# Token-layout projections of 512 columns and score products of 128 rows in a two-block attention network

## The chip, the cores and the metric

The kernel runs on one core of a Trainium2 chip. Its time is the device time of one execution in microseconds (us). The engines are TensorE (PE, matmuls; PEld its weight loads), VectorE (DVE), ScalarE (ACT), GpSimd (POOL) and SyncE (SP, which issues nearly all DMAs). All run side by side, each in its own order, and wait for one another by semaphores.

## The reference

The input is one sequence of 512 tokens with 1024 channels. Two different blocks of two layers each follow one another. Cut to what matters here:

```python
# first block, per layer
h = x @ w_in[i]                       # q, k, v of three attentions, and three gates
o_fox = fox_attention(fq, fk, fv, log_f)       # 6 heads of 64, a cumulated forget gate in the logits
o_sb  = stick_breaking_attention(sq, sk, sv)   # 5 heads of 64
o_dsa = dsa_attention(dq, dk, dv, iq, ik, iw)  # 5 heads of 64, on the 256 best keys
merged = gates0 * (o_fox @ w_up_fox[i]) + gates1 * (o_sb @ w_up_sb[i]) + gates2 * (o_dsa @ w_up_dsa[i])
x = layer_norm(ALPHA * x + merged @ w_out[i])
ffn = square(relu(x @ w_ff_in[i])) @ w_ff_out[i]               # 4096 hidden channels
ple = sigmoid(x @ w_ple_gate[i]) * (p[i] @ w_ple[i])
x = layer_norm(ALPHA * x + ffn + ple)
# second block, per layer
mixed = concatenate([y_nsa * silu(z_nsa), y_lru * silu(z_lru), y_conv * silu(z_conv)])   # 3 x 512 channels
x = x + mixed @ w_out_2[l]                                     # then an RMS norm
```

In the forget-gate attention the logits of query q and key k are `q.k / 8 + c[q] - c[k]`, where c is the running sum of the log gates.

## The kernel before, in words

Every operand of a large matmul is held as two tiles, a rounded high part and the low remainder. `mm3` (L209) multiplies high by high, high by low and low by high into one PSUM bank, so each k-tile of 128 channels takes three passes (L212 to L214).

Two layouts are in use. In the channel layout (`w_tiles`, L239) 128 columns of the weight stand in the array and all 512 tokens move, so each pass has 512 columns. In the token layout (`t_groups`, L262) 128 tokens of the activation stand in the array and the weight's columns move. A group of columns is loaded as slabs of four k-tiles by 256 columns (`slab`, L216), split by ScalarE and VectorE or GpSimd (`wsplit`, L235), and then each block of 128 tokens goes through all k-tiles before the next block starts.

The token layout serves five places: the attention output (`out1`, L822), the side gate and its partner `w_ple` (L876 to L891), the four chunks of the feed-forward output (L924), and the second block's output (`out2`, L1510). In all of them 1024 output columns are taken in four quarters of 256. `out_groups` (L858) takes the first two quarters one by one and the last two together, so that the last two share one walk over the token blocks and the norm of block b can start when block b is done. The residual tile of a quarter comes from `quarter` (L855). VectorE adds each quarter from PSUM, takes its statistics (`bn_stats`), and behind the last quarter `norm_out` (L795) norms the block and transposes it for the next stage.

The score products are in `scores` (L312): `q` and `k` are lists of operands that are multiplied pairwise. `head_pairs` (L534) makes them for the forget-gate and stick-breaking heads. A query tile holds the high part in 64 rows and the low part in the other 64 (`query_stack`, L417), a key tile the high part twice (`key_stack`, L434), and the key's low part is a separate half tile of 64 rows, two heads to a tile (`low`). So one pass has 128 rows and a second one has 64. The forget gate adds a third product between them, of 38 rows (L731). Where an attention has five heads, the up-projection of `branch` (L669) has a last k-tile of 64 channels: it takes one pass of 128 rows (L693, the weight's high part above its low part) and one of 64 rows (L694).

The program is written in order of dependence; the framework orders each engine's instructions itself, by a simulated time line, and mixes stages where data and buffers allow. The numbers of buffers are fixed in `BUFS` (L89) and `PBUFS` (L107): 13 `qk` tiles in the first block, four `wh` and four `wl` slabs, four `raw` slabs, and PSUM banks under the names `mm` (3), `ss` (2), `tr` (2), `av` and `acc` (1 each). `ORDER` (L103) gives the stages of a first-block layer: index, selection, forget-gate project, sparse project, forget-gate attend, best keys, sparse attend, branch of the forget gate (x), stick-breaking project and attend, and the branches of sparse (z) and stick-breaking (y).

Of the kernel before, what the change touches and what calls it, by code (L numbers as in the profile page):

```python
# [11 lines left out]
F32 = mybir.dt.float32  # L12
# [18 lines left out]
def _shape_constants():  # L31
# [14 lines left out]
    for h in range(6):  # L46
        sel[h::32, h] = 1.0
    cast = [mask(i[None, :] <= i[:, None]), mask(i[None, :] // 64 <= i[:, None] // 64),
# [21 lines left out]
class Net:  # L70
# [26 lines left out]
    COMMON = ["wh", "wl"]  # L97
    WORDS = dict(s=512, rs=512, tmp=256, raw=1024, wh=1024, wl=1024)
    SIDE = 9
# [162 lines left out]
    def t_groups(self, w, groups, x, emit, K=KD, ks=4, first=None, then=None):  # L262
# [6 lines left out]
        for b in range(NT):  # L269
            tok = slice(b * P, (b + 1) * P)  # L270
            for g, cols in enumerate(groups):
# [9 lines left out]
                emit(b, g, ps[:, :n])  # L281


    def transpose_block(self, src, b, xh, xl, kd=KD):
# [149 lines left out]
    def key_stack(self, ps, z, lo, r):  # L434

        nc = self.nc
        hi = z[r:r + 64]
        nc.scalar.activation(hi, ps[r:r + 64], AF.Copy)
        self.lo_engine().tensor_sub(lo, ps[r:r + 64], hi.bitcast(F32))
        nc.scalar.activation(z[64 - r:128 - r], ps[r:r + 64], AF.Copy)  # L440

    def index_project(self, w, x, then):
# [91 lines left out]
    def head_pairs(self, w, tiles, x):  # L534


        q, k, lows = {}, {}, []

        def low(j):
            if j % 2 == 0:  # L540
                lows.append(self.t("qk", [P, 2, T], F32R))
            return lows[-1][:, j % 2]

        def emit(i, ps):
            j = i // 2
            ps = self.staged(ps)
            t = self.t("qk", [P, 2, T], F32R)
            if i % 2 == 0 and i == len(tiles) - 1:
                z, l = t[:, 0], low(j)[:64]
                self.query_stack(ps, z, 0, 0)  # L550
                self.key_stack(ps, t[:, 1], l, 64)
                q[2 * j], k[2 * j] = (z, z[:64]), (t[:, 1], l)
                return
            l = low(j) if i % 2 else None
            for r in range(2):
                rows, h = slice(64 * r, 64 * r + 64), 2 * j + r
                z = t[:, r]
                if i % 2:
                    self.key_stack(ps, z, l[rows], 64 * r)
                    k[h] = z, l[rows]  # L560
                else:
                    self.query_stack(ps, z, 64 * r, 64 * r)
                    q[h] = z, z[rows]

        self.w_tiles(w, tiles, x, emit)
        return q, k
# [66 lines left out]
    def attend(self, n_heads, v, probs):  # L633


        pairs = []
        for j in range((n_heads + 1) // 2):
            o = self.t("os", [P, T])
            nr = min(2, n_heads - 2 * j)
            for r in range(nr):  # L640
                h = 2 * j + r
                for half in range(2):
                    av = self.ps("av")[:, :256]
                    self.unit(half, lambda b, s, p: probs(h, b, s, p), v(h), av)
# [24 lines left out]
    def branch(self, w, g0, wup, pairs, rows, x, emit):  # L669
# [6 lines left out]
        def gate(f, ps):  # L676
# [25 lines left out]
    def mix1(self, i, x, then=None):  # L702
# [88 lines left out]
    def stats(self):  # L791

        return [self.small([P, 4, 6]) for _ in range(NT)]

# [27 lines left out]
    def out1(self, i, merged, xd):  # L822
# [10 lines left out]
        def add(j):  # L833
            def emit(b, k, ps):
                v = self.quarter(y, b, j + k)
                nc.vector.scalar_tensor_tensor(v, v, ALPHA, ps, op0=OP.mult, op1=OP.add)
                nc.vector.bn_stats(st[b][:, j + k], v)
                if j + k == 3:
                    self.norm_out(y[b], b, st[b], g, bb, 1e-5, x)
            return emit  # L840

        self.out_groups(a["w_out"][i], m, add)
        return x, y
# [9 lines left out]

    @staticmethod
    def quarter(y, b, j):  # L855
        return y[b][j // 2][:, j % 2 * 256:j % 2 * 256 + 256]

    def out_groups(self, w, x, add, K=KD):  # L858
# [14 lines left out]
    def ffn(self, i, x, y, pt, post=None):  # L873
        nc = self.nc
        a = self.a
        for j in range(4):  # L876
            cols = [(j * 256, 256)]
            wh, wl = self.wpair(self.slab(a["w_ple"][i], cols, 0, 2))

            def emit(b, ps):  # L880
                s = self.t("tmp", [P, 256])
                nc.scalar.activation(s, ps, AF.Tanh, scale=0.5)
                u = self.ps("mm")[:, :256]
# [4 lines left out]
                v = self.quarter(y, b, j)  # L888
                nc.vector.scalar_tensor_tensor(v, v, ALPHA, s, op0=OP.mult, op1=OP.add)

            self.t_group(a["w_ple_gate"][i], cols, x, emit)  # L891
        xo = self.xpair()
        xn = self.dram([T, D])
        nch = 4
        for ch in range(nch):
# [18 lines left out]
            def add(j):  # L914
                def emit(b, k, ps):
                    v = self.quarter(y, b, j + k)
                    nc.vector.tensor_add(v, v, ps)
                    if last:
                        nc.vector.bn_stats(st[b][:, j + k], v)
                    if last and j + k == 3:  # L920
# [589 lines left out]
    def out2(self, l, mixed, xd):  # L1510
# [10 lines left out]
        def add(j):  # L1521
            def emit(b, k, ps):
                v = self.quarter(y, b, j + k)
                nc.vector.tensor_add(v, v, ps)
                nc.vector.bn_stats(st[b][:, j + k], v)
                if j + k == 3:
                    rows = slice(b * P, (b + 1) * P)
# [10 lines left out]
        self.lo_on_pool = False  # L1538
        for j in range(4):
            self.t_groups(a["w_out"][l], [[(j * 256, 256)]], m, add(j), K=12)  # L1540
        return h, xn
# [77 lines left out]
```

## Time and profile before

| what | value |
|---|---|
| median of 3 runs | 2654.8 us (2652.48 to 2656.91) |
| profiled execution, its own time | 2650.83 us |
| its span, first to last instruction | 2649.0 us |
| mean granted TensorE clock in the span | 0.98 of 2.4 GHz |
| busy: PE, DVE, ACT, POOL | 97%, 62%, 45%, 29% |
| PE instructions | 15636 |
| DMA, mean | 89 GB/s |

All times below are from the one profiled execution, counted from its first instruction. A row of the time line gives the start in us, the duration in us, engine, line, operation, tiles (`out<-in`), the form (rows*columns of the array, then the moving operand) and how many instructions of the kind follow one another. Matmuls are pipelined and their ends are modelled: the price of one is read from the starts, not from the durations. A stretch of the view by windows gives the busy time of each engine, its instructions in brackets, the granted clock of TensorE (1.00 is 2.4 GHz, 0.50 is 1.2 GHz), the share of the DMA engines and GB/s.

### The profile page before, as it was taken

To read this page: it belongs to the slowest core of one execution; us is meant where nothing else is said; L and a number is where in the kernel's file an instruction comes from. 1 tells how busy PE (TensorE), PEld (TensorE's weight loads), DVE (VectorE), ACT (ScalarE), POOL (GpSimd) and SP (SyncE) were. 2 spreads that over 40 slices of the span, in tenths; PEclk is the share of its full clock that TensorE was granted. 3 is DMA by queue.
4 is the path that set the end of the run, shared out by engine and by line. 5 is a ranking of instruction groups with operands and counts; after the bars stand their busy time and mean duration, and the time that the engine had idled before them with its cause. 6 is when DMAs were issued, how large, how long until landed. Compare 5 with 4: busy or idle time off the path is not lost.

```text
span 2649.0 us, 40689 instructions
## 1 busy us (share of the span) xinstructions
PE 2577.2 (97%) x15636; PEld 2272.5 (86%) x15636; DVE 1651.1 (62%) x3306; ACT 1179.9 (45%) x2229; POOL 765.5 (29%) x853
## 2 busy tenths in 40 slices
PE   8999999999999999999999999998999989999988
PEld 8878878989988987787799889988987679988678
DVE  4975665643344669657565443346699765699764
ACT  5655543232233255555323332233675742566750
POOL 6621352000000264205100000004596322587330
PEclk9989999999999998999999999999999999999999
DMA  5202225232233332122432323133512034522140
GB/s 168 74 15 75 78 68 172 84 110 90 80 104 96 103 82 66 45 81 63 135 120 85 112 93 114 58 109 105 136 45 70 27 101 125 143 68 68 34 141 33
DMA packets 256642, 236.84 MB, mean 89 GB/s; under 512 B 23168, under 2 KB 245696, under 8 KB 256448
## 3 DMA queue, kind: packets, MB, share of 16 engines
q1 hardware_dynamic: 256448, 234.25, 29.5%
q8 instruction: 123, 2.02, 0.3%
q14 instruction: 71, 0.58, 0.1%
HBM read 224.51 MB, written 9.70 MB: 88 GB/s over the span
## 4 chain that ended last, share of the span: by engine, by line
PE 85%; DVE 10%; ACT 3%; issue 1%; POOL 1%; DMA 0%; DVEq 0%; POOLq 0%; SPq 0%; ACTq 0%
PE mm L212 24%; PE mm L213 24%; PE mm L214 24%; PE ss L317 3%; PE av L367 3%; PE tr L352 2%; DVE acc L1350 1%; DVE s L324 1%; PE tr L360 1%; DVE sc L492 1%; PE ss L731 1%; PE tr L413 1%; DVE m L491 1%; PE av L1178 1%; PE mm L694 1%
## 5 line engine op out<-in xcount | busy, mean ns | idle before, releaser
L236 ACT ACTIVATE wh<-raw 128x1024 fp32r<-128x1024 f32 (+3 forms) x418 | 414.2, 995 | 553.7 <-PE mm L214 372.7
L212 PE MATMUL mm<-xt,wh 128*128 128x512 f32 x1456 | 576.6, 396 | 7.2 <-ACT sig L1394 4.9
L213 PE MATMUL mm<-xt,wh 128*128 128x512 f32 x1456 | 576.6, 396 | 0.0
L214 PE MATMUL mm<-xt,wl 128*128 128x512 f32 x1456 | 573.1, 394 | 0.0
L237 DVE TENSOR_TENSOR wl<-raw,wh 128x1024 fp32r<-128x1024 f32 (+3 forms) x312 | 374.5, 1202 | 208.8 <-ACT wh L236 203.9
L213 PE MATMUL mm<-wl,qk 128*128 128x256 f32 x1728 | 485.7, 283 | 0.0
L214 PE MATMUL mm<-wh,qk 128*128 128x256 f32 x1728 | 485.2, 283 | 0.0
L212 PE MATMUL mm<-wh,qk 128*128 128x256 f32 x1728 | 485.0, 284 | 0.0
L213 PEld LDWEIGHTS mm<-wl,qk 128*128 128x128 f32 x1728 | 330.3, 192 | 0.5
L212 PEld LDWEIGHTS mm<-xt,wh 128*128 128x128 f32 x1456 | 276.0, 190 | 63.7 <-ACT sig L1394 5.4
L214 PEld LDWEIGHTS mm<-wh,qk 128*128 128x128 f32 x1728 | 330.5, 192 | 0.0
L212 PEld LDWEIGHTS mm<-wh,qk 128*128 128x128 f32 x1728 | 329.6, 192 | 0.5
L214 PEld LDWEIGHTS mm<-xt,wl 128*128 128x128 f32 x1456 | 275.6, 189 | 56.4 <-issue 1.6
L213 PEld LDWEIGHTS mm<-xt,wh 128*128 128x128 f32 x1456 | 276.1, 190 | 55.4 <-issue 1.8
L299 POOL TENSOR_SCALAR tiny<-tiny 128x1 f32<-128x1 f32 x24 | 13.3, 554 | 1002.0 <-DVE tiny L801 982.5
L237 POOL TENSOR_TENSOR wl<-raw,wh 128x1024 fp32r<-128x1024 f32 (+7 forms) x106 | 233.0, 2205 | 159.1 <-ACT wh L236 157.0
L212 PE MATMUL mm<-wh,xt 128*128 128x256 f32 (+5 forms) x880 | 263.0, 304 | 6.5 <-ACT wh L236 6.4
L214 PE MATMUL mm<-wh,xt 128*128 128x256 f32 (+6 forms) x880 | 264.4, 302 | 3.8 <-DVE xt L205 3.8
L213 PE MATMUL mm<-wl,xt 128*128 128x256 f32 (+6 forms) x880 | 265.5, 304 | 1.8 <-DVE wl L237 1.2
L212 PEld LDWEIGHTS mm<-wh,xt 128*128 128x128 f32 x880 | 169.6, 195 | 9.0 <-ACT wh L236 6.4
L214 PEld LDWEIGHTS mm<-wh,xt 128*128 128x128 f32 x880 | 170.5, 194 | 5.6 <-DVE xt L205 4.4
L213 PEld LDWEIGHTS mm<-wl,xt 128*128 128x128 f32 x880 | 170.8, 194 | 4.5 <-DVE wl L237 1.7
(321 smaller groups left out, 4181.5 us busy)
## 6 DMA issues: line engine op xcount, KB each, us to landing
raw<-in_w_in SPq DMA_DIRECT2D x84, 512.0 KB, 3.8
raw<-in_w_ff_in SPq DMA_DIRECT2D x64, 512.0 KB, 4.9
raw<-in_w_ff_out SPq DMA_DIRECT2D x64, 512.0 KB, 3.5
raw<-in_w_in SPq DMA_DIRECT2D x104, 256.0 KB, 3.3
raw<-in_w_out SPq DMA_DIRECT2D x40, 512.0 KB, 3.9
raw<-in_w_ple_gate SPq DMA_DIRECT2D x16, 512.0 KB, 4.1
raw<-in_cmp_w SPq DMA_DIRECT2D x16, 512.0 KB, 5.0
spill<-ac SPq DMA_DIRECT2D x24, 256.0 KB, 2.1
```

The source lines that it names most:

```text
L212: mm(out, A[0], B[0], start=start, stop=False)
L213: mm(out, A[0], B[1], start=False, stop=False)
L214: mm(out, A[1], B[0], start=False, stop=stop)
L236: self.nc.scalar.activation(hi, raw, AF.Copy)
L237: (self.nc.gpsimd if self.lo_on_pool else self.nc.vector).tensor_sub(lo, raw, hi.bitcast(F32))
L317: self.nc.tensor.matmul(s, u[:, tok], v[:, :n], start=i == 0, stop=i == len(k) - 1)
L324: nc.vector.tensor_tensor_reduce(p, s, bias, -0.125, 3e38, OP.add, OP.min, m)
L352: nc.tensor.transpose(tr[:, kb * P:(kb + 1) * P], p[:, kb * P:(kb + 1) * P], self.ident)
L360: nc.tensor.transpose(tr[:, i * P:(i + 1) * P], src, self.ident)
L367: nc.tensor.matmul(av[:, 256 - m.shape[-1]:], v[:, kb], m, start=start and kb + i == 0, stop=stop and kb == n - 1 and i == 1)
L413: nc.tensor.transpose(tr[:, i * P:(i + 1) * P], z[:, i].rearrange("p a d -> p (a d)"), self.identr)
L491: nc.vector.max(m8, sc)
```

## The change

The token layout gets a new walk, `wide`. It takes 512 columns at a time, slabs of two k-tiles by 512 columns, and one PSUM bank for each of the four token blocks (the banks named in `WIDE`). The first k-pairs are walked with the pair outside and the four blocks inside; the last `stay` pairs are held together and walked block by block, and each block is emitted when it is done. `out_halves` replaces `out_groups`: the first half of the columns with one pair held, the second with four. For eight k-tiles four pairs are all, so the second half is walked block by block in the `mm` banks. The side gate and `w_ple` take two halves as well. The adds and statistics on VectorE take 512 columns at once, the tile of the side gate comes from `sig` instead of `tmp`, and `quarter` is gone.

The second operand of the scores is made 128 rows high: `key_stack` copies the low part of the key into the other 64 rows too, and the second product takes the whole query tile. Each head now has a key tile of its own beside the query tile that two heads share. The forget-gate product takes all 128 rows, with a selector that has ones at two rows only. The last k-tile of an up-projection with five heads takes 128 rows in both passes; its `pairs` tile gets high and low parts copied into the lower half. The words of a `ph` tile go from 384 to 512.

```diff
     sel = np.zeros((P, 6))
     for h in range(6):
-        sel[h::32, h] = 1.0
+        sel[[h, 32 + h], h] = 1.0
...
-    WORDS = dict(s=512, rs=512, tmp=256, raw=1024, wh=1024, wl=1024)
+    WORDS = dict(ph=512, s=512, rs=512, tmp=256, raw=1024, wh=1024, wl=1024)
...
+    WIDE = ("av", "ss", "ss", "tr")
+
+    def wide(self, w, c0, x, emit, K=KD, stay=4):
+        pairs = list(range(0, K, 2))
+        first, last = pairs[:-stay], pairs[-stay:]
+        cols = [(c0, T)]
+        banks = [self.ps(t) for t in self.WIDE] if first else None
+
+        def add(ps, b, k0, slab):
+            tok = slice(b * P, (b + 1) * P)
+            h, l = slab
+            for k in (k0, k0 + 1):
+                self.mm3(ps, (x[0][:, k, tok], x[1][:, k, tok]), (h[:, k - k0], l[:, k - k0]), k == 0, k == K - 1)
+
+        for k0 in first:
+            slab = self.wpair(self.slab(w, cols, k0, 2))
+            for b in range(NT):
+                add(banks[b], b, k0, slab)
+        slabs = [self.wpair(self.slab(w, cols, k0, 2)) for k0 in last]
+        for b in range(NT):
+            ps = banks[b] if first else self.ps("mm")
+            for k0, slab in zip(last, slabs):
+                add(ps, b, k0, slab)
+            emit(b, ps)
...
         nc.scalar.activation(hi, ps[r:r + 64], AF.Copy)
-        self.lo_engine().tensor_sub(lo, ps[r:r + 64], hi.bitcast(F32))
+        self.lo_engine().tensor_sub(lo[r:r + 64], ps[r:r + 64], hi.bitcast(F32))
         nc.scalar.activation(z[64 - r:128 - r], ps[r:r + 64], AF.Copy)
+        nc.scalar.activation(lo[64 - r:128 - r], lo[r:r + 64].bitcast(F32), AF.Copy)
...
+        def pair():
+            t = self.t("qk", [P, 2, T], F32R)
+            return t[:, 0], t[:, 1]
 
         def emit(i, ps):
             j = i // 2
             ps = self.staged(ps)
...
+            if i % 2:
+                for r in range(2):
+                    k[2 * j + r] = pair()
+                    self.key_stack(ps, *k[2 * j + r], 64 * r)
                 return
...
+            z = pair()
+            last = i == len(tiles) - 1
+            for r in range(1 if last else 2):
+                self.query_stack(ps, z[r], 64 * r, 64 * r)
+                q[2 * j + r] = z[r], z[r]
+            if last:
+                k[2 * j] = pair()
+                self.key_stack(ps, *k[2 * j], 64)
...
             if nr == 1:
-                self.nc.scalar.activation(t[64:, 0], t[:64, 0].bitcast(F32), AF.Copy)
+                self.nc.scalar.activation(t[64:], t[:64].bitcast(F32), AF.Copy)
...
-                nc.tensor.matmul(u, h[:64, full, c], pairs[full][:64, 1], start=False, stop=False)
+                nc.tensor.matmul(u, h[:, full, c], pairs[full][:, 1], start=False, stop=False)
...
-                    r = slice(64 * (h % 2), 64 * (h % 2) + 38)
-                    nc.tensor.matmul(s, self.sel[r, h:h + 1].to_broadcast([38, P]), c[r, :n],
+                    nc.tensor.matmul(s, self.sel[:, h:h + 1].to_broadcast([P, P]), c[:, :n],
                                      start=False, stop=False)
...
-        cols = [[(j * 256, 256)] for j in range(4)]
-        for j in range(2):
-            self.t_groups(w, [cols[j]], x, add(j), K)
-        self.t_groups(w, cols[2:], x, add(2), K)
+    def out_halves(self, w, x, add, K=KD):
+
+        self.wide(w, 0, x, add(0), K, stay=1)
+        self.wide(w, T, x, add(1), K)
...
-            self.t_group(a["w_ple_gate"][i], cols, x, emit)
+            self.wide(a["w_ple_gate"][i], j * T, x, emit, stay=1)
...
-            self.out_groups(a["w_ff_out"][i][ch * D:(ch + 1) * D], m, add)
+            self.out_halves(a["w_ff_out"][i][ch * D:(ch + 1) * D], m, add)
...
-        for j in range(4):
-            self.t_groups(a["w_out"][l], [[(j * 256, 256)]], m, add(j), K=12)
+        self.out_halves(a["w_out"][l], m, add, K=12)
```

## Rows read from the trace of the kernel before

**Rows 1.** The page, busy time by engine and the chain that ended last.

```profile
PE 2577.2 (97%) x15636; PEld 2272.5 (86%) x15636; DVE 1651.1 (62%) x3306; ACT 1179.9 (45%) x2229; POOL 765.5 (29%) x853
...
PE 85%; DVE 10%; ACT 3%; issue 1%; POOL 1%; DMA 0%; DVEq 0%; POOLq 0%; SPq 0%; ACTq 0%
```

**Rows 2.** Busy time by stretch: engines, granted clock, DMA share, GB/s.

```profile
440.00:900.00 460.00, 460.00 (x3153) 429.86 (x3152) 218.59 (x327) 133.92 (x173) 9.23 (x12) 1.00 0.31 96
100.00:130.00 30.00, 30.00 (x157) 25.51 (x155) 28.83 (x77) 15.80 (x41) 17.03 (x24) 1.00 0.30 84
131.00:159.00 28.00, 27.57 (x89) 20.72 (x90) 23.18 (x71) 11.97 (x34) 5.68 (x11) 0.51 0.00 1
159.00:190.00 31.00, 30.69 (x160) 23.21 (x160) 18.92 (x58) 17.33 (x44) 6.03 (x12) 1.00 0.10 30
285.00:360.00 75.00, 75.00 (x368) 58.20 (x367) 56.41 (x91) 41.25 (x93) 41.71 (x63) 1.00 0.20 56
```

**Rows 3.** PE by line and form: count, busy us, mean ns, idle before.

```profile
L212 PE MATMUL mm<-xt,wh 128*128 128x512 f32 x1456 | 576.6, 396 | 7.2 <-ACT sig L1394 4.9 <-DVE sig L1314 1.8 <-DVE cg L1385 0.6
...
L213 PE MATMUL mm<-wl,qk 128*128 128x256 f32 x1728 | 485.7, 283 | 0.0
...
L694 PE MATMUL mm<-qk,wh 64*128 64x512 f32 x32 | 15.9, 497 | 0.0
...
L317 PE MATMUL ss<-qk,qk 64*128 64x512 f32 x22 | 10.6, 481 | 0.0
```

**Rows 4.** PE in order of time, from the up-projections into the attention output.

```profile
439.95 0.39 PE L212 MATMUL mm<-qk,wh 128*128 128x512 f32 x1
...
440.63 0.28 PE L212 MATMUL mm<-wh,qk 128*128 128x256 f32 x1
...
445.90 0.28 PE L214 MATMUL mm<-wh,qk 128*128 128x256 f32 x1
```

**Rows 5.** PE in order of time, an up-projection and a stick-breaking score pair.

```profile
299.55 0.39 PE L693 MATMUL mm<-qk,wh 128*128 128x512 f32 x1
299.87 0.50 PE L694 MATMUL mm<-qk,wh 64*128 64x512 f32 x1
300.29 0.92 PE L317 MATMUL ss<-qk,qk 128*128 128x512 f32 x2
301.15 0.50 PE L212 MATMUL mm<-qk,wh 128*128 128x512 f32 x1
301.48 0.39 PE L213 MATMUL mm<-qk,wh 128*128 128x512 f32 x1
```

**Rows 6.** PE in order of time, token layout with 448 columns.

```profile
96.71 0.36 PE L212 MATMUL mm<-wh,xt 128*128 128x448 f32 x1
...
98.94 0.37 PE L214 MATMUL mm<-wh,xt 128*128 128x448 f32 x1
```

**Rows 7.** PE in order of time, forget-gate scores; L731, L317 and L212 lie between.

```profile
176.11 0.40 PE L317 MATMUL ss<-qk,qk 128*128 128x512 f32 x1
...
177.43 0.39 PE L213 MATMUL mm<-qk,wh 128*128 128x512 f32 x1
```

**Rows 8.** PE in order of time, sparse scores, two products of 128 rows.

```profile
196.68 0.62 PE L317 MATMUL ss<-q,q 128*128 128x512 f32 x2
197.14 0.27 PE L360 MATMUL tr<-kept,s 128*128 128x128 f32 x1
```

**Rows 9.** ACT and POOL by line and form, key copies of the forget-gate heads.

```profile
L440 ACT ACTIVATE qk<-s 64x512 fp32r<-64x512 f32 x12 | 7.6, 630 | 0.3
...
L439 POOL TENSOR_TENSOR qk<-s,qk 64x512 fp32r<-64x512 f32 x12 | 15.5, 1291 | 1.2 <-ACT qk L438 0.8
```

**Rows 10.** DVE in order of time, the last add of the kernel.

```profile
2641.74 0.42 DVE L1524 TENSOR_TENSOR ac<-ac,mm 128x256 f32<-128x256 f32 x1 [0.52 <-PE mm L214]
```

**Rows 11.** The page, weight splits: mean ns, idle before and its releaser.

```profile
L236 ACT ACTIVATE wh<-raw 128x1024 fp32r<-128x1024 f32 (+3 forms) x418 | 414.2, 995 | 553.7 <-PE mm L214 372.7
...
L237 DVE TENSOR_TENSOR wl<-raw,wh 128x1024 fp32r<-128x1024 f32 (+3 forms) x312 | 374.5, 1202 | 208.8 <-ACT wh L236 203.9
```

More of the change, by code (lines that the diff above doesn't have):

```diff
@@ L534, in head_pairs @@
     def head_pairs(self, w, tiles, x):
[L537 to L542, printed above, removed]
+        q, k = {}, {}
+        def pair():
+            t = self.t("qk", [P, 2, T], F32R)
+            return t[:, 0], t[:, 1]
         def emit(i, ps):
@@ L546, in emit @@
             ps = self.staged(ps)
[L547 to L552, printed above, removed]
-                return
[L554 to L563, printed above, removed]
+            if i % 2:
+                for r in range(2):
+                    k[2 * j + r] = pair()
+                    self.key_stack(ps, *k[2 * j + r], 64 * r)
+                return
+            z = pair()
[6 more added lines that the diff above has]
+                self.key_stack(ps, *k[2 * j], 64)
         self.w_tiles(w, tiles, x, emit)
@@ L791, in stats @@
     def stats(self):
-        return [self.small([P, 4, 6]) for _ in range(NT)]
+        return [self.small([P, 2, 6]) for _ in range(NT)]
     def norm_out(self, y, b, stats, g, bb, eps, x, xd=None, post=None):
@@ L833, in add, with emit @@
         def add(j):
-            def emit(b, k, ps):
-                v = self.quarter(y, b, j + k)
+            def emit(b, ps):
+                v = y[b][j]
                 nc.vector.scalar_tensor_tensor(v, v, ALPHA, ps, op0=OP.mult, op1=OP.add)
-                nc.vector.bn_stats(st[b][:, j + k], v)
-                if j + k == 3:
+                nc.vector.bn_stats(st[b][:, j], v)
+                if j == 1:
                     self.norm_out(y[b], b, st[b], g, bb, 1e-5, x)
             return emit
-        self.out_groups(a["w_out"][i], m, add)
+        self.out_halves(a["w_out"][i], m, add)
         return x, y
@@ L852, in residual @@
         return y
[L854 to L858, printed above, removed]
-        cols = [[(j * 256, 256)] for j in range(4)]
-        for j in range(2):
-            self.t_groups(w, [cols[j]], x, add(j), K)
-        self.t_groups(w, cols[2:], x, add(2), K)
+    def out_halves(self, w, x, add, K=KD):
+        self.wide(w, 0, x, add(0), K, stay=1)
+        self.wide(w, T, x, add(1), K)
     def ple_input(self, i):
@@ L875, in ffn @@
         a = self.a
-        for j in range(4):
-            cols = [(j * 256, 256)]
-            wh, wl = self.wpair(self.slab(a["w_ple"][i], cols, 0, 2))
+        ple = {}
+        for j in range(2):
             def emit(b, ps):
-                s = self.t("tmp", [P, 256])
+                if b == 0:
+                    ple[j] = self.wpair(self.slab(a["w_ple"][i], [(j * T, T)], 0, 2))
+                wh, wl = ple[j]
+                s = self.t("sig", [P, T])
                 nc.scalar.activation(s, ps, AF.Tanh, scale=0.5)
-                u = self.ps("mm")[:, :256]
+                u = self.ps("mm")
                 tok = slice(b * P, (b + 1) * P)
@@ L887, in emit @@
                 nc.vector.scalar_tensor_tensor(s, s, 1.0, u, op0=OP.add, op1=OP.mult)
-                v = self.quarter(y, b, j)
+                v = y[b][j]
                 nc.vector.scalar_tensor_tensor(v, v, ALPHA, s, op0=OP.mult, op1=OP.add)
-            self.t_group(a["w_ple_gate"][i], cols, x, emit)
+            self.wide(a["w_ple_gate"][i], j * T, x, emit, stay=1)
         xo = self.xpair()
@@ L914, in add, with emit @@
             def add(j):
-                def emit(b, k, ps):
-                    v = self.quarter(y, b, j + k)
+                def emit(b, ps):
+                    v = y[b][j]
                     nc.vector.tensor_add(v, v, ps)
                     if last:
-                        nc.vector.bn_stats(st[b][:, j + k], v)
-                    if last and j + k == 3:
+                        nc.vector.bn_stats(st[b][:, j], v)
+                    if last and j == 1:
                         self.norm_out(y[b], b, st[b], g, bb, 1e-5, xo, xn, post)
                 return emit
-            self.out_groups(a["w_ff_out"][i][ch * D:(ch + 1) * D], m, add)
+            self.out_halves(a["w_ff_out"][i][ch * D:(ch + 1) * D], m, add)
         return xo, xn
@@ L1521, in add, with emit @@
         def add(j):
-            def emit(b, k, ps):
-                v = self.quarter(y, b, j + k)
+            def emit(b, ps):
+                v = y[b][j]
                 nc.vector.tensor_add(v, v, ps)
-                nc.vector.bn_stats(st[b][:, j + k], v)
-                if j + k == 3:
+                nc.vector.bn_stats(st[b][:, j], v)
+                if j == 1:
                     rows = slice(b * P, (b + 1) * P)
@@ L1538, in out2 @@
         self.lo_on_pool = False
-        for j in range(4):
-            self.t_groups(a["w_out"][l], [[(j * 256, 256)]], m, add(j), K=12)
+        self.out_halves(a["w_out"][l], m, add, K=12)
         return h, xn
```

## The prediction

> **What bounds the kernel now.** I read the page first: TensorE (PE) is busy 97% of the span and holds 85% of the chain that ended last [rows 1]. Then the stretches: from 440 to 900 us PE is busy for all of 460 us, in 285:360 for all of 75 us, while VectorE (DVE) has room; in 100:130 PE and DVE are both nearly full; in 131:159 PE is full at a granted clock of 0.51, that is mostly at 1.2 GHz [rows 2]. A pipelined PE looks busy even where it waits, so I went on to start times. The duration of a pass (396 ns at 512 columns, 283 ns at 256) is not its price, because passes overlap [rows 3]. The price is the distance from one start to the next. At a seam between two stages three 512-column passes start 439.95 to 440.63, 226.7 ns each, and the 44 passes of 256 columns up to 445.90 take 5.27 us, 119.8 ns each [rows 4]. Two narrow ones cost 239.6 ns, so each wide one that replaces two saves 12.9 ns: 256 more columns add only 106.9 ns, and some 13 ns are paid per pass. The last thing read is what passes of fewer than 128 rows do to that rhythm: the product of 64 rows in the up-projections starts 0.32 us after the one ahead, the next 0.42 us later [rows 5].
>
> **Wide projections.** Passes replaced, per layer of the first block: attention output 8 k-tiles x 4 token blocks x 4 quarters x 3 = 384, the four feed-forward outputs 1536, the side gate 384, its partner with two k-tiles 96: 2400, two layers 4800. The second block's output has 12 k-tiles: 576, twice 1152. Together 5952 of 256 columns become 2976 of 512. All but the gate's 768 multiply a `qk` tile: 5184, three lines of 1728, of which one stands in the rows [rows 3]. Saving 2976 x 12.9 ns = 38.4 us, nearly all of it in stretches where PE is full and nothing else is late. The 512-column rows have the activations moving; in the token layout the widest is 448 columns, eleven distances in 2.23 us, 202.7 ns [rows 6]. Carried on from 256 at that slope (0.432 ns a column), 512 would cost 230.3 ns and the saving is 27.7 us. I take 38.4, since the column count is the same as in the rows of 226.7 ns, and keep 27.7 as the low end. "TensorE: Matmul & The Clock Gate" in the Trainium skill (Back-to-back issue gap) has a pass at its columns over 2.4 GHz plus 2.5 ns; by that the merge would be worth 7.4 us as an estimate and the whole sum 49 us. The rows show a constant five times as large, and they decide.
>
> **Full rows.** (a) Up-projections of 320 rows: 32 products of 64 rows [rows 3]. From L693 at 299.55 to 301.48 lie five distances, 1.93 us where full-row ones would take 5 x 0.2267 = 1.13; these five hold one up-projection pair and one stick-breaking pair, so 0.40 us each [rows 5]. 32 x 0.40 = 12.8 us. (b) Stick-breaking: 5 heads x 4 blocks x 2 layers = 40 pairs, 16.0 us. (c) Forget-gate attention: 48 triples (128, 38, 64 rows), which with (b) make the 88 score products of 64 rows, 22 of each width [rows 3]. L317 at 176.11 to L213 at 177.43 is four distances in 1.32 us against 0.91: 0.41 us, 19.7 us in all [rows 7]. As a control, two full-row score products take 0.46 us, nothing over 2 x 0.23 [rows 8]. (a) and (b) lie where PE is full and DVE is not. In (c) DVE is at 28.83 of 30 in 100:130, 23.18 of 28 in 131:159, 18.92 of 31 in 159:190 [rows 2]; if DVE set the pace, none of the 19.7 would show, if PE does, all. PE is full in all three and DVE in one of them, so I take 15.
>
> **What is added.** Each of 22 keys and 4 single-head outputs gets one more copy of 64x512 on ScalarE, 0.63 us by the same kind of copy [rows 9]: 16.4 us on an engine that is busy 45% [rows 1]. Hidden by the matmuls that PE has queued; with that cover gone, all 16.4. In the forget-gate stage the copy must wait for GpSimd's subtraction, 1.29 us [rows 9]; behind it in ScalarE's order stand the next head's copies and weight splits, and 12 such waits are at most 15.5 us, on ScalarE and not on PE. Heads take one `qk` tile more (9 for 8, 8 for 7); with 3 value tiles and 3 outputs still held, the stick-breaking stage would like 14 of 13, so one tile waits for the last branch. At best that costs nothing, as that branch's matmuls must run anyway. At worst the stage loses its fill: 368 passes in 75 us now, at the pace of 131:159 (89 in 28) 116 us, 41 more per layer [rows 2]. I take nothing, as PE is now full there.
>
> **What moves.** The four accumulators now go through the k-pairs side by side, so the last token block of the normed input is wanted 18 wide passes (4.1 us) into the side gate, not three blocks of 24 narrow passes (8.6 us). If nothing is pulled ahead, PE stalls up to 4.5 us, twice; if passes of other blocks are, zero. The rows show different products interleaved pass by pass [rows 5, 7], so zero. Weight slabs keep their bytes (two k-tiles by 512 columns for four by 256) and their count, so splits and DMAs are the same in number, with rows twice as long. DVE adds once per 512 columns instead of twice per 256; behind the last matmul of a layer the add (0.42 us at 256 columns [rows 10]) and the statistics grow by between nothing and that much each, 0 to 0.84 us. Four such ends are uncovered, and with some 0.5 at each: +2.
>
> **Sum.** -38.4 - 12.8 - 16.0 - 15 + 2 = -80.2 us. The profiled execution took 2650.83 (span 2649.0 and 1.8 around it), so 2570.6; the median of the runs is 4.0 higher, and against it I expect 2575.
>
> **Rivals.**
> 1. Half of it (chance 0.24). The wide pass costs 230 ns, DVE hides (c), the copies show: -27.7 - 28.8 + 2 + 16.4 = -38, 2617; with only some of these, 2590 to 2617. For it: DVE's load in 100:130. Against: PE full in all stretches.
> 2. The half-speed stretch goes too (0.10). 89 instructions take 28 us there and would take 17 at the pace of 100:130 [rows 2], 11 us per layer, 22 in all: 2553. Full rows keep the array busier; against it, the softmax chain around them stays.
> 3. Nothing to save (0.05). A wide pass costs exactly two narrow ones and the delays of short rows pass to the transposes beside them; with the longer ends, 2657, no change. Speaking against it: the seam, and the control without any delay [rows 4, 8]. The same page (its last section, on why this matters) says that a single product of 32 rows takes the time of 128 rows, and by that padding would gain nothing; the 0.32 and 0.42 us beside 0.23 disagree [rows 5].
> 4. Slower (0.07): weight slabs become the bound. The second half of an output holds four slabs at once, and there are four buffers. If they turn over only as a set, PE waits for four splits, ScalarE 1.0 and DVE 4 x 1.2 us [rows 11], before the half and again behind it: 11.6 us, in 12 such halves 139 us, 2714. It decides from 80 us on, seven halves. Against it: two groups of two slabs are held in the same way now, and PE is full over those 460 us [rows 2].
>
> **Numbers.** The forecast has 0.54. The range runs 2548 to 2614: from rival 2's value to nearly rival 1's full sum; it leaves out 3, 4 and the ends of 1 and 2, some 0.18. A measurement of this kernel tells about 0.2% (5 us) from no change. Faster: forecast, 1 and 2, 0.88; same: 3, 0.05; slower: 4, 0.07.
>
> **What would show it.** The changed profile should have 12,660 PE instructions (15636 - 2976), no 256-column group on `qk`, and starts 227 ns apart there; no group of 38 or 64 rows in the scores or up-projections, and full-row products at 0.23 us behind one another; each of the five output stretches of a first-block layer shorter by 5% with PE still full. Each L440 copy has a second one behind it, with no new idle time of PE. Wrong would be: PE waiting on weight splits in the output stages (rival 4), starts at 230 ns or more or a forget-gate stage as long as now (rival 1), a stick-breaking stage with PE idle.

## The result, and the profile after

The changed kernel takes 2575.46 us (median of 4 runs, 2573.60 to 2577.27) where the kernel before takes 2653.66 beside it (4 runs): ratio 0.970, 95% interval 0.9687 to 0.972, so 78 us are gone. The forecast was 2575. The profiled execution took 2573.6 us, its span is 2571.6. The page of the changed kernel, busy time by engine, the chain that ended last by engine, and the weight splits (L236, L237):

```profile
PE 2485.1 (97%) x12660; PEld 2106.2 (82%) x12660; DVE 1625.2 (63%) x3126; ACT 1187.9 (46%) x2231; POOL 756.9 (29%) x853
...
PE 22%; DVE 7%; ACT 2%; issue 1%; POOL 0%; DVEq 0%; POOLq 0%; ACTq 0%
...
L236 ACT ACTIVATE wh<-raw 128x1024 fp32r<-128x1024 f32 (+6 forms) x414 | 414.5, 1003 | 586.3 <-PE tr L214 230.5
...
L237 DVE TENSOR_TENSOR wl<-raw,wh 128x1024 fp32r<-128x1024 f32 (+3 forms) x308 | 371.3, 1206 | 326.3 <-ACT wh L236 316.8
```

Against [rows 1]: PE has the 12,660 instructions that the forecast counted, and is still busy 97%. The chain's shares add up to a third of the span here and to all of it before, so its 22% is not to be set against the 85%; the stretches below say what bounds. The splits are as long as in [rows 11] and four fewer on ScalarE and on VectorE, since a slab of the side gate's partner, which has only two k-tiles, now holds 512 columns.

PE by line and form in the changed kernel: the output products of 512 columns, the second product of an up-projection (L717), the forget gate's product (L753) and the score products (L344).

```profile
L213 PE MATMUL mm<-wl,qk 128*128 128x512 f32 x352 | 136.2, 390 | 0.0
...
L212 PE MATMUL ss<-wh,qk 128*128 128x512 f32 x256 | 99.6, 389 | 0.0
...
L344 PE MATMUL ss<-qk,qk 128*128 128x512 f32 x44 | 16.9, 422 | 0.0
...
L717 PE MATMUL mm<-qk,wh 128*128 128x512 f32 x32 | 12.6, 395 | 0.0
...
L753 PE MATMUL ss<-kept 128*128 128x512 f32 x12 | 4.7, 392 | 0.0
```

The 256-column groups on `qk` and the 64-row groups of [rows 3] are gone; every score product and every up-projection has 128 rows. What a pass costs is read from starts. PE of the changed kernel in order of time, first in a feed-forward output, then an up-projection, then a forget-gate triple and the transpose behind it:

```profile
564.76 0.39 PE L214 MATMUL ss<-wh,qk 128*128 128x512 f32 x1
...
567.48 0.39 PE L214 MATMUL tr<-wh,qk 128*128 128x512 f32 x1
...
291.27 0.39 PE L716 MATMUL mm<-qk,wh 128*128 128x512 f32 x1
291.49 0.39 PE L717 MATMUL mm<-qk,wh 128*128 128x512 f32 x1
291.72 0.39 PE L212 MATMUL mm<-qk,wh 128*128 128x512 f32 x1
291.95 0.28 PE L394 MATMUL av<-pt,qk 128*128 128x256 f32 x1
...
173.31 0.40 PE L344 MATMUL ss<-qk,qk 128*128 128x512 f32 x1
173.54 0.39 PE L753 MATMUL ss<-kept 128*128 128x512 f32 x1
173.77 0.39 PE L344 MATMUL ss<-qk,qk 128*128 128x512 f32 x1
174.00 0.27 PE L387 MATMUL tr<-kept,s 128*128 128x128 f32 x1
```

Twelve wide passes from 564.76 to 567.48 take 2.72 us, 226.7 ns each, across a change of PSUM bank (`ss` to `tr`). The up-projection's three distances take 0.68 us, the triple's three 0.69: the delays of [rows 5, 7] are nowhere.

The stretches of the changed kernel (length, busy time and count of PE, PEld, DVE, ACT and POOL, granted clock, DMA share, GB/s):

```profile
417.00:867.00 450.00, 450.00 (x2007) 372.78 (x2006) 212.55 (x262) 134.80 (x166) 8.64 (x14) 1.00 0.32 99
100.00:130.00 30.00, 29.57 (x159) 25.64 (x157) 29.54 (x78) 17.41 (x42) 16.36 (x25) 1.00 0.34 97
131.00:159.00 28.00, 24.38 (x130) 19.98 (x131) 27.23 (x82) 15.86 (x42) 6.39 (x12) 0.94 0.05 16
270.00:325.00 55.00, 54.70 (x319) 48.16 (x319) 50.39 (x82) 36.05 (x88) 38.73 (x59) 1.00 0.21 60
...
1012.00:1036.00 24.00, 20.75 (x107) 17.06 (x105) 16.81 (x50) 11.82 (x29) 4.63 (x9) 0.93 0.15 39
```

Against [rows 2]: the outputs and the feed-forward keep PE full for all of 450 us; the stick-breaking stage (270:325) keeps it full too. The stretch from 131 to 159 is another one now: the clock is 0.94 where it was 0.51, PE does 130 instructions where it did 89, and DVE, 27.23 of 28, has become the busiest engine there. The last row is a stretch of the same stage in the second layer.

To place the gain, the span is cut at the first and the last output pass of each layer (starts of the L212 passes on `wh` and `qk`, the first of each three, from the time line), which gives sums for the mixes of attention in the first block, its outputs with the feed-forward, the mixes and the outputs of the second block, and what comes behind the last pass:

| us | mixes 1 | outputs 1 | mixes 2 | outputs 2 | end | span |
|---|---|---|---|---|---|---|
| before | 878.7 | 933.1 | 690.1 | 139.3 | 7.8 | 2649.0 |
| after | 839.8 | 899.1 | 683.1 | 140.7 | 8.9 | 2571.6 |
| wide walk, split passes | 834.8 | 932.1 | 684.8 | 149.8 | 8.5 | 2610.0 |
| full rows only | 833.0 | 933.1 | 698.8 | 139.1 | 7.8 | 2611.8 |
| wide only | 880.6 | 899.1 | 684.1 | 140.5 | 8.9 | 2613.2 |
| short scores | 872.5 | 899.2 | 695.4 | 140.6 | 8.9 | 2616.6 |
| short stick-breaking | 851.4 | 899.2 | 683.9 | 140.5 | 9.0 | 2584.0 |
| short forget gate | 855.8 | 899.3 | 691.6 | 140.5 | 8.9 | 2596.1 |
| short up-projections | 851.0 | 899.2 | 683.3 | 140.6 | 8.9 | 2583.0 |
| old output of block 2 | 841.4 | 899.1 | 701.3 | 139.2 | 8.1 | 2589.1 |
| convolution first | 838.7 | 899.2 | 697.1 | 129.7 | 8.9 | 2573.6 |
| short scores, no copies | 874.5 | 899.1 | 684.8 | 140.5 | 8.9 | 2607.8 |
| short gate product only | 857.4 | 899.2 | 693.1 | 140.5 | 8.9 | 2599.1 |
| 14 `qk` tiles | 838.0 | 899.2 | 689.3 | 140.6 | 8.9 | 2576.0 |

Of the 77.4 us between the two spans, 38.9 left the first block's mixes, 34.0 its outputs, 7.0 the second block's mixes; its outputs and the end grew by 2.5. Two cautions are in the table. The mixes of the second block run from 683.1 to 695.4 in the nine kernels that have the changed kernel's code for that block (all but before, split passes, full rows only, old output and convolution first). And the first block's mixes, with the same code in six kernels (after, split passes, full rows only, old output, convolution first, and 14 tiles but for their number), run from 833.0 to 841.4. So an edit is read from its own stage, and even there a few us are not its own.

### The profile page after: what moved, and what is told of

Same layout as the page of the kernel before. It is cut to its first block, busy times and chain, and to the rows that moved or that the text cites. A ratio compares the mean times of both kernels' runs of the same rounds, so it can differ in the third digit from the quotient of the medians.

```text
span 2571.6 us, 34737 instructions
## 1 busy us (share of the span) xinstructions
PE 2485.1 (97%) x12660; PEld 2106.2 (82%) x12660; DVE 1625.2 (63%) x3126; ACT 1187.9 (46%) x2231; POOL 756.9 (29%) x853
## 5 line engine op out<-in xcount | busy, mean ns | idle before, releaser
L236 ACT ACTIVATE wh<-raw 128x1024 fp32r<-128x1024 f32 (+6 forms) x414 | 414.5, 1003 | 586.3 <-PE tr L214 230.5
L212 PE MATMUL mm<-xt,wh 128*128 128x512 f32 x1456 | 575.6, 395 | 4.2 <-ACT sig L1411 3.5
L237 DVE TENSOR_TENSOR wl<-raw,wh 128x1024 fp32r<-128x1024 f32 (+3 forms) x308 | 371.3, 1206 | 326.3 <-ACT wh L236 316.8
L212 PEld LDWEIGHTS mm<-xt,wh 128*128 128x128 f32 x1456 | 275.4, 189 | 59.8 <-ACT sig L1411 4.0
L326 POOL TENSOR_SCALAR tiny<-tiny 128x1 f32<-128x1 f32 x24 | 12.2, 508 | 985.9 <-DVE tiny L823 966.5
L237 POOL TENSOR_TENSOR wl<-raw,wh 128x1024 fp32r<-128x1024 f32 (+7 forms) x106 | 231.3, 2189 | 85.6 <-ACT wh L236 82.1
L212 PE MATMUL mm<-wh,xt 128*128 128x256 f32 (+6 forms) x624 | 191.7, 314 | 7.8 <-ACT wh L236 6.5
L214 PE MATMUL mm<-wh,xt 128*128 128x256 f32 (+6 forms) x624 | 193.6, 312 | 5.3 <-DVE xt L205 5.3
L213 PE MATMUL mm<-wl,xt 128*128 128x256 f32 (+6 forms) x624 | 193.9, 313 | 1.3 <-DVE wl L237 0.7
L353 ACT ACTIVATE s<-s,tm 128x128 f32<-128x128 f32 (+1 forms) x216 | 120.8, 559 | 100.4 <-DVE tm L351 92.2
L213 PE MATMUL mm<-wl,qk 128*128 128x512 f32 x352 | 136.2, 390 | 0.0
L214 PE MATMUL mm<-wh,qk 128*128 128x512 f32 x352 | 136.0, 389 | 0.0
L212 PE MATMUL mm<-wh,qk 128*128 128x512 f32 x352 | 134.7, 389 | 0.0
L212 PEld LDWEIGHTS mm<-wh,xt 128*128 128x128 f32 x624 | 121.2, 196 | 10.2 <-ACT wh L236 6.5
L214 PEld LDWEIGHTS mm<-wh,xt 128*128 128x128 f32 x624 | 122.1, 196 | 7.4 <-DVE xt L205 6.2
L213 PEld LDWEIGHTS mm<-wl,xt 128*128 128x128 f32 x624 | 122.3, 196 | 3.9 <-POOL wl L237 1.3
L1367 DVE SCALAR_TENSOR_TENSOR acc<-cu,kept,acc 128x511 f32<-128x511 f32 (+6 forms) x168 | 123.8, 737 | 1.5
L356 POOL TENSOR_SCALAR s<-s,tm,kept 128x128 f32<-128x128 f32 (+3 forms) x128 | 80.9, 633 | 90.1 <-DVE tm L355 82.0
```

Source lines behind the costliest of these rows:

```text
L212: mm(out, A[0], B[0], start=start, stop=False)
L213: mm(out, A[0], B[1], start=False, stop=False)
L214: mm(out, A[1], B[0], start=False, stop=stop)
L236: self.nc.scalar.activation(hi, raw, AF.Copy)
L237: (self.nc.gpsimd if self.lo_on_pool else self.nc.vector).tensor_sub(lo, raw, hi.bitcast(F32))
L353: nc.scalar.activation(p, p, AF.Exp, bias=m, scale=-1.0, accum_out=den)
```

## The experiments

### Which half brings what

Theory: the gain of the wide projections is the constant of about 13 ns that each pass pays, and the rows of the short products bring the rest by their delays. First the whole wide walk, slabs, banks, adds and statistics of the changed kernel, with each pass of 512 columns issued as two of 256:

```diff
-                self.mm3(ps, (x[0][:, k, tok], x[1][:, k, tok]), (h[:, k - k0], l[:, k - k0]), k == 0, k == K - 1)
+                for c in (slice(0, 256), slice(256, 512)):
+                    self.mm3(ps[:, c], (x[0][:, k, tok], x[1][:, k, tok]), (h[:, k - k0, c], l[:, k - k0, c]),
+                             k == 0 and c.start == 0, k == K - 1 and c.start == 256)
```

> The changed kernel with every 512-column pass of the new walk issued as two passes of 256 columns; walk, slabs, banks and adds stay. If each pass pays a constant of some 13 ns (main theory), 2976 more passes cost 38 us: 2614 us, starts 120 ns apart. If the walk itself gave the gain (k-pairs outside, fewer VectorE adds, longer DMA rows), the time stays at 2575 to 2582. By the 2.5 ns a pass of the page's formula it would be 2583.

Measured: 2614.50 us, ratio to before 0.9855 (0.9839 to 0.9872), 39.0 above the changed kernel. PE of this kernel in order of time, in a feed-forward output:

```profile
585.03 0.28 PE L212 MATMUL av<-wh,qk 128*128 128x256 f32 x1
...
586.47 0.28 PE L212 MATMUL ss<-wh,qk 128*128 128x256 f32 x1
```

Twelve distances in 1.44 us, 120 ns, as in [rows 4]. The outputs of the first block are back at 932.1. 39.0 us over 2976 passes saved is 13.1 ns each. So the walk itself, the larger adds and the longer slabs bring nothing that shows; the number of passes is all of it, to within the few us by which the runs of one kernel differ.

Then each half of the change alone, from the kernel before: the full rows (`key_stack`, `head_pairs`, `sel`, the forget-gate product and the lines in `attend` and `branch`), and the wide projections without them.

> The kernel before with the full-row products alone. Main theory: the delays around 88 score pairs or triples and 32 up-projection products go, 0.40 us each and the forget gate at three quarters: 44 us, 2610 us on the scale where the kernel before has 2654. If padding rows is worth nothing, 2654 or, with the added copies showing, up to 2670.

> The changed kernel with the old score and up-projection products, so the wide projections alone. Main theory: 38 us less than before, 2616 us; the gains of this run and of the full-row run then add up to the 78 us of both. If the two share a cause (a better order, or a clock that falls less), they add up to clearly more or less than that, by over 15 us.

Measured: full rows only 2614.09 us, 0.9857 (0.984 to 0.9873), 39.8 gained; wide only 2615.92, 0.9862 (0.9847 to 0.9877), 38.0 gained. Together that is 77.8 for the 78.2 of both, so within a few us neither takes from the other. The split kernel above, with the new walk, and the full rows alone, with the old one, issue the same number of passes and take 2614.50 and 2614.09 us.

### The full rows, one at a time

All of these start from the changed kernel. First both kinds of score products short again, tiles and copies as they are:

```diff
-                self.scores(s, q[h], k[h], b)
+                self.scores(s, *half(q[h], k[h], h), b)
...
+def half(q, k, h):
+    r = slice(64 * (h % 2), 64 * (h % 2) + 64)
+    return (q[0], q[1][r]), (k[0], k[1][r])
```

with the same call in the forget gate, and its own product short:

```diff
-        sel[[h, 32 + h], h] = 1.0
+        sel[h::32, h] = 1.0
...
-                    nc.tensor.matmul(s, self.sel[:, h:h + 1].to_broadcast([P, P]), c[:, :n],
+                    r = slice(64 * (h % 2), 64 * (h % 2) + 38)
+                    nc.tensor.matmul(s, self.sel[r, h:h + 1].to_broadcast([38, P]), c[r, :n],
```

> The changed kernel with the second score product of forget-gate and stick-breaking heads back on 64 rows and the gate's product on 38 rows; tiles and the added copies stay. Main theory: 16 us for the 40 stick-breaking pairs and 15 (if VectorE hides a part) to 20 us for the 48 triples come back: 2606 to 2611 us. If the delay does not come from the row count, 2575. If VectorE set the pace in the forget-gate stage, only the 16: 2591.

Measured: 2615.24 us, 0.986 (0.9845 to 0.9874), 39.8 above the changed kernel, more than expected. The profiled execution is 45.0 longer: 32.7 in its own stages, the first block's mixes, and 12.3 in the second block's, whose code is that of the changed kernel. So the two were taken apart, and the up-projections (`h[:64, full, c], pairs[full][:64, 1]` again) with them.

> The changed kernel with only the second stick-breaking product back on 64 rows. Main theory: 40 pairs at 0.40 us, 16 us, 2591 us, all of it between 260 and 330 us and its like in layer two; the clock of the forget-gate stage does not change. If the short products of this stage had lowered the clock of the other, a half-speed stretch of some 27 us would be back.

> The changed kernel with only the forget-gate triple back on 128, 38 and 64 rows. Delay theory: 48 times 0.41 us, 15 to 20 us, 2591 to 2595 us, with the clock as now. Clock theory: the short products also bring back the half-speed stretch (27 us in each layer in the kernel before and in the run with all score products short, 3 to 10 us now), and the time rises by more than the delays, 20 to 30 us, 2595 to 2605 us. With both short runs together 40 us is to be shared out.

> The changed kernel with only the second up-projection product back on 64 rows. Main theory: 32 products at 0.40 us, 12.8 us, 2588 us. If the delays of one stage hide behind other work, less: the stage table leaves only some 4 us a layer for it, 2579 to 2584.

Measured: stick-breaking 2586.26 us, 0.9754 (0.9737 to 0.9772), +10.8; forget gate 2599.65, 0.9798 (0.9784 to 0.9813), +24.2; up-projections 2585.51, 0.9745 (0.9731 to 0.976), +10.0. In the first block's mixes the three are +11.6, +16.0 and +11.2: 38.8, about the 38.9 that left them, each with the scatter of some 8 us that the table shows.

Up-projections and stick-breaking behave as delays at a full clock. With short stick-breaking products, PE in order of time shows a pair standing alone and two pairs behind one another:

```profile
290.81 0.39 PE L212 MATMUL mm<-xt,wh 128*128 128x512 f32 x1
291.03 0.81 PE L344 MATMUL ss<-qk,qk 128*128 128x512 f32 x2
291.77 0.50 PE L213 MATMUL mm<-xt,wh 128*128 128x512 f32 x1
292.11 0.39 PE L214 MATMUL mm<-xt,wl 128*128 128x512 f32 x1
292.34 0.47 PE L344 MATMUL ss<-qk,qk 128*128 128x128 f32 x2
292.75 0.50 PE L212 MATMUL mm<-xt,wh 128*128 128x512 f32 x1
293.08 0.40 PE L213 MATMUL mm<-xt,wh 128*128 128x512 f32 x1
...
303.45 1.40 PE L344 MATMUL ss<-qk,qk 128*128 128x512 f32 x4
304.79 0.50 PE L213 MATMUL mm<-xt,wh 128*128 128x512 f32 x1
305.12 0.39 PE L214 MATMUL mm<-xt,wl 128*128 128x512 f32 x1
```

and the changed kernel, in the same view, the same products with full rows:

```profile
290.35 0.33 PE L344 MATMUL ss<-qk,qk 128*128 128x128 f32 x2
290.52 0.45 PE L212 MATMUL mm<-xt,wh 128*128 128x512 f32 x1
290.81 0.39 PE L213 MATMUL mm<-xt,wh 128*128 128x512 f32 x1
...
300.38 0.87 PE L344 MATMUL ss<-qk,qk 128*128 128x512 f32 x4
301.09 0.45 PE L213 MATMUL mm<-xt,wh 128*128 128x512 f32 x1
301.37 0.39 PE L214 MATMUL mm<-xt,wl 128*128 128x512 f32 x1
```

The pair of 512 columns costs 0.39 us over four plain distances (290.81 to 292.11 against 0.91), which is the forecast's 0.40. The pair of 128 columns takes 0.74 us (292.34 to 293.08) and still 0.46 with full rows: 0.28 saved. Two pairs in a row with the pass behind them take 1.67 against 0.99, 0.34 a pair.

In the forget gate the clock changes too. The stretch of 131:159 with its products short:

```profile
131.00:159.00 28.00, 26.98 (x90) 19.36 (x90) 22.70 (x72) 11.58 (x34) 6.04 (x11) 0.57 0.00 1
1012.00:1036.00 24.00, 23.53 (x76) 17.19 (x77) 21.42 (x70) 9.52 (x26) 4.28 (x8) 0.53 0.00 1
```

The clock is back near its lower level (0.57; 0.50 is 1.2 GHz), and PE back at 90 instructions in 28 us; the second stretch, in the second layer, has 0.53 where the changed kernel has 0.93. Delay or clock? One short product in each triple, the gate's own, with both score products full, halves the number of short products and was meant to halve the delays:

> The changed kernel with the forget gate's own product back on 38 rows, the second score product full. If each change of the row count costs PE its delay and nothing else, two of the three delays of a triple come back, some 13 of 20 us at most, 2585 us, with the half-speed stretch as short as now. If the short rows are what lets the clock fall, the stretch of 24 to 27 us is back and the time is 2590 to 2600 us.

Measured: 2604.49 us, 0.9822 (0.9799 to 0.9845), 29.0 above the changed kernel. In the profiled execution the first block's mixes are 17.6 longer, and the second block's, with the same code as the changed kernel's, 10.0. Its stretches:

```profile
131.00:159.00 28.00, 26.75 (x82) 19.76 (x82) 23.61 (x74) 11.65 (x34) 6.01 (x11) 0.51 0.00 1
1012.00:1036.00 24.00, 23.30 (x73) 17.29 (x73) 22.00 (x76) 10.96 (x30) 5.33 (x10) 0.51 0.00 0
```

Half the short products cost as much as all of them, and the clock is as low. That does not set delay and clock apart, for PE in order of time shows that the delays were not halved. With both products short a triple in the second layer reads:

```profile
1041.56 0.39 PE L344 MATMUL ss<-qk,qk 128*128 128x512 f32 x1
1041.87 0.49 PE L754 MATMUL ss<-kept 38*128 38x512 f32 x1
1042.20 0.40 PE L344 MATMUL ss<-qk,qk 64*128 64x512 f32 x1
...
1042.87 0.22 PE L344 MATMUL ss<-qk,qk 128*128 128x128 f32 x1
```

and the same triple with the gate's product alone short:

```profile
1043.03 0.39 PE L344 MATMUL ss<-qk,qk 128*128 128x512 f32 x1
1043.35 0.49 PE L754 MATMUL ss<-kept 38*128 38x512 f32 x1
1043.77 0.50 PE L344 MATMUL ss<-qk,qk 128*128 128x512 f32 x1
1044.11 0.39 PE L214 MATMUL mm<-qk,wl 128*128 128x512 f32 x1
1044.34 0.22 PE L344 MATMUL ss<-qk,qk 128*128 128x128 f32 x1
```

From the first line to the last there are four distances, and either way they take 1.31 us, 0.40 over four plain ones. A second short product behind the first adds nothing: the delay belongs to the step from full rows to short ones and back. So the expectation's two delays of three were miscounted, and the run keeps all of the delay and all of the low clock. It shows that the gate's own product is enough to bring both back; how the stage's 16 to 18 us are shared between them stays open. In 131:159 the granted clock is 0.51 to 0.76 in all six kernels with short gate products (before, wide only, short scores with and without copies, and these two) and 0.88 to 0.94 in the other eight.

### What was costed at nothing

The added copies: the kernel with short scores does not need the copy of the key's low part into the other rows (but for a single last head), so here it is left out.

```diff
-        nc.scalar.activation(lo[64 - r:128 - r], lo[r:r + 64].bitcast(F32), AF.Copy)
+        if copy:
+            nc.scalar.activation(lo[64 - r:128 - r], lo[r:r + 64].bitcast(F32), AF.Copy)
```

> The run with short score products (2615 us) without the added copies of the keys' low parts, which those products do not read (two of 22 stay). If the copies are hidden, as the sum has it, 2615 us; if ScalarE's extra 12.6 us or the waits for GpSimd show, down to 2600.

Measured: 2610.64 us, 0.984 (0.9824 to 0.9856), 4.6 below the kernel with copies. But the mixes in which the copies stand are no shorter, 874.5 against 872.5; the difference lies in the second block, whose code has no such copy. So no cost of the copies shows, to within the scatter of these mixes; the row of them in the changed kernel (ACT by line and form) says how many and how long:

```profile
L468 ACT ACTIVATE qk<-qk 64x512 fp32r<-64x512 f32 x22 | 13.8, 627 | 8.1 <-POOL qk L466 8.0
```

ScalarE waits 8.0 us in all for GpSimd's subtraction, before 11 of the 22, and no idle time of PE before a score product is put down to the copies. The stick-breaking stage's missing tile, `qk=14` for 13:

> The changed kernel with 14 instead of 13 of the tiles that queries, keys and values share. If the missing tile holds up the stick-breaking stage, it gets shorter and the time falls by 3 us or more; if the last branch's matmuls fill the gap, as the sum has it, 2575 give or take 3.

Measured: 2577.97 us, 0.9714 (0.9696 to 0.9733), nothing gained: the shortage costs nothing that shows.

### The second block's output

Its outputs got no shorter (139.3 to 140.7), which looked as if 1152 narrow passes had become 576 wide ones for nothing. Two readings: the wide passes bring nothing there, or something of the same length moved in. First the old walk there, by quarters of 256 columns, the rest as changed:

```diff
-        self.out_halves(a["w_out"][l], m, add, K=12)
+        for j in range(4):
+            self.t_groups(a["w_out"][l], [[(j * 256, 256)]], m, add(j), K=12)
```

> The changed kernel with the second block's output back in four quarters of 256 columns, the rest as it is. By the count of passes 576 at 12.9 ns come back, 7.4 us: 2583 us. By the stage table, where the two output stages last 70.6 and 70.1 us after 70.5 and 68.8 before, nothing comes back or 1 to 3 us are gained: 2572 to 2576.

Measured: 2587.69 us, 0.9756 (0.9741 to 0.9771), 12.2 above the changed kernel, so the guess from the stages fell. How much the passes pay, this run does not say: by their count it is 7.4, and the mixes in front, 18.2 longer here, differ by up to 12.3 between kernels with the same code. Then the new walk with the four k-tiles of the convolution first, so that nothing of the output can start before they are there:

```diff
+        if K == 12:
+            pairs = pairs[4:] + pairs[:4]
```

(with the start and stop of the accumulation at the first and last of these pairs).

> The changed kernel with the k-pairs of the second block's output walked in another order, the convolution's last two pairs first. With the quarters back, 12 us had come back where the passes alone account for 7.4. If the other 5 are passes that the wide walk can begin before the convolution's output is there, they are lost here too, since no pass can begin early: 2580 us. If it is only the order that the stage happened to get, 2575 give or take 3.

Measured: 2575.85 us, 0.9709 (0.9694 to 0.9724), no change. The outputs now take 65.1 and 64.6 us (288 x 0.2267 is 65.3), 129.7 in sum where the narrow passes of the kernel before take 139.3, and the mixes in front of them are longer by 14.0 in sum. So the wide passes do take less time there, but in the changed kernel they start early, among the last passes of the mix, and the stage looks 5 us long for that. A boundary that work can cross is no measure of its stage.

## Why the prediction was right

**Wide projections.** The forecast was 38.4 us; measured 38.0 alone, 39.0 by splitting, 38.6 as the difference of both to the full rows alone (2614.09 - 2575.46). Reading the price from the starts at the seam [rows 4] was the step that carried it. The low end, a slope from 448 columns [rows 6], fell: passes of 448 columns still take 203 ns in the changed kernel and those of 512 take 226.7, not 230.3. The 7.4 us by the formula of "TensorE: Matmul & The Clock Gate" in the Trainium skill (Back-to-back issue gap) fell with it: that formula is for a matmul by itself, and here, where each pass has weights of its own, the split kernel measures 13.1 ns a pass, not 2.5.

**Full rows.** Forecast 43.8, measured 39.8 alone and 40.5 on top of the wide passes. (a) Up-projections: 12.8 forecast, 11.2 in their stage; in the trace of the short up-projections the starts around the 32 products lie 12.4 us behind plain distances in sum, 0.39 each. (b) Stick-breaking: 16.0 forecast, 11.6 in its stage. The step that was too large is the one price of 0.40 us for all 40 pairs: it came from 512 columns, and narrow pairs and pairs in a row save 0.28 to 0.34. Summed over all 40 pairs, the same distances take 13.2 us longer in the trace with short pairs than in that of the changed kernel, 0.33 a pair; that is 2.8 of the 4.4 us, and the other 1.6 lie within the scatter of the stage. (c) Forget gate: 15 taken of 19.7, 16.0 in its stage, and that agreement is partly luck. The forecast asked whether PE or DVE sets the pace there and set rival 2, the clock, beside it. The runs have both at once: the delay of a triple is as forecast at a full clock (0.40 for 0.41), the low clock comes with the short rows, and with full rows DVE (27.23 of 28) is the busiest engine. The stage's 16.0 (forget gate short) or 17.6 (gate product short) hold delay and clock together, and no run has the one without the other. That is why rival 2's premise came true without its 22 us: they do not come on top of (c).

**The rest.** Copies, tile and the order of the side gate were costed at nothing. The first two cost nothing that shows in the runs, though the scatter of the mixes could hide up to some 8 us of copies; of the third, PE without a gap over 417:867, where it stands, says the same. Rival 4, the slabs, falls by that line, and rival 3 by the 38.0 and 39.8 us of the two halves alone. The end was taken at 0.5 each; the last one costs 1.1 us (8.9 against 7.8). DVE of the changed kernel in order of time, the last add and the statistics behind it:

```profile
2563.54 0.69 DVE L1541 TENSOR_TENSOR ac<-ac,tr 128x512 f32<-128x512 f32 x1 [1.17 <-PE tr L214]
2564.26 0.69 DVE L1542 BATCH_NORM_STATS2 tiny<-ac 128x6 f32<-128x512 f32 x1
```

The add takes 0.69 us for 0.42 in [rows 10], the statistics 0.69 for 0.43: 0.53 in all, about what was taken. The other half of the 1.1 is not in DVE's two instructions; part of it is that the last k-tile's passes, from whose first one the end is counted, are themselves wide.

**Why the total fits better than the terms.** That the median agrees to half a us is luck. Between the profiled executions 77.2 us went (2650.83 to 2573.6) where the sum has 80.2; the median agrees to half a us because the profiled execution stands only 1.9 below the median after, and 4.0 was carried over from before. Within the sum (a) and (b) were 6.0 too large, (c) 1.0 too small, the first block's outputs 3.0 too small (34.0 where 2400 x 12.9 ns is 31.0; what the 3.0 are stays open). The second block gave 5.6, its mixes 7.0 and its outputs -1.4, where its 576 passes saved stand in the sum with 7.4.

## What to carry to other kernels

Price a matmul by the distance of starts in a stretch where PE is full, and count passes: 512 columns in one pass instead of two saved 13 ns each, whatever else was rebuilt around them. A product of few rows among full ones delays its neighbours, by 0.3 to 0.4 us a pair here, and in a thin stretch the clock was low with it, so filling the array's rows, with copies or zeros, is worth trying where the copies that it needs lie on an engine with room. Read an edit from its own stage, since where the framework orders the whole program, a stage of unchanged code moved by more than 10 us between kernels.

## What was not expected of the hardware

One product of 38 rows in each forget-gate triple, twelve of each width in the whole kernel, is enough to bring TensorE back near 1.2 GHz for most of the thin stretch in both layers (0.51 in 131:159 and in 1012:1036), and with all rows full it is granted 0.94 and 0.93. Beside passes of the projections the same triples did not lower the clock: in 100:130 five of them run at a granted 1.00 with short rows and with full ones. What does this, the few rows or the delays that come with them, the runs do not tell. PE looks busier with the low clock (26.75 of 28) than with the high one (24.38), since each pass lasts longer and a delay counts as busy (0.49 us for the pass of 38 rows at 1043.35, 0.39 for that of 128 at 173.54), so its busy share is as much effect as cause. "TensorE: Matmul & The Clock Gate" in the Trainium skill (HAM oscillation) puts a falling clock down to idle gaps of PE; here the kernel with less idle time in the profile has the lower clock, but as the profile books delays as busy, the trace neither bears that out nor speaks against it.

The delay of a short product at a full clock is not its own: it starts 0.1 us late, the next full one 0.2 us late again, and the one behind that another 0.1 (0.32, 0.42 and 0.34 us from 1043.03 on, for 0.23). "TensorEngine Tiling (Array Packing)" (Key Properties) in the Trainium skill says that a change of tiling mode drains the engine; the rows agree with a cost at each change, 0.39 us for a pair standing alone, and with none between products of 128 rows or from 38 rows to 64.
